# Down projection of an expert layer in column ranges of 512, 512, 384, 384, 256, gate products spread between pinned pairs of expert batches, and SBUF pools at other byte offsets

## The chip, the cores and the metric

The kernel runs on one NeuronCore of a Trainium2 chip. The metric is the device time of one execution in microseconds (us), the median of a few runs. Engines are named as the profile names them: PE is TensorE (matmuls; PEld its weight loads), DVE is VectorE, ACT is ScalarE, POOL is GpSimd, SP is SyncE, which only issues DMAs. SBUF is the on-chip memory that the engines read operands from, 128 partitions wide; PSUM is the small memory that PE accumulates into.

## The reference, cut to what matters

The program is two transformer blocks on 256 tokens of 2048 features. The first block (adaptive norm, three token mixers, a SwiGLU layer) and the mixer of the second are touched only by where their buffers lie. What the change rewrites is the end of the second block: a hierarchical mixture of 32 experts, and a gate on the whole residual.

```python
def hierarchical_moe(hn, w_router_group, w_router_expert, w_gate, w_up, w_down):
    ...   # group of the token, two experts in it, their weights: comb (tokens x 32)
    for e in range(N_EXPERTS):
        hid = jax.nn.silu(t @ w_gate[e]) * (t @ w_up[e])
        out = out + (hid @ w_down[e]).astype(jnp.float32) * comb[:, e:e + 1]

        h = h + hierarchical_moe(hn, ...)
        gate = jax.nn.sigmoid(rms_norm_2(h, ple_norm[i]) @ w_ple_gate[i])
        h = h + gate * (p[i] @ w_ple_up[i])
    return h
```

`w_down` is 32 x 256 x 2048 and `w_ple_gate` is 2048 x 2048, all fp32.

## The kernel before

**Dense layers.** Most of the time goes to products of fp32 data in three passes. `split` (lines 190 to 192) makes a rounded copy `whi` of a weight tile on ACT and the rest `wlo` on DVE; PE then adds `whi` by `xhi`, `wlo` by `xhi` and `whi` by `xlo` (lines 86, 87, 88), each a matmul of 128x128 stationary by 128x512 moving in the type fp32r. The stationary operand is the activations (`xhi`, `xlo`), the moving one the weights. In the output layer of the first block's feed-forward part the stationary tiles are called `hhi` and `hlo` and lie in another pool than all the others.

**Pools.** A pool with `side="right"` is laid down from the top of SBUF, the others from the bottom. The split weights, `xhi` and `xlo` and the weight buffers `w` lie in right pools; `hhi`, `hlo`, the expert weights `we` and the small scratch tiles (`junk`) in left ones. In the kernel before, the right pools start 480 bytes past a multiple of 512, the left ones 384.

**Router.** After the last column group of `w_out_2`, `residual_by4` adds the residual (L1227) and writes the sum `xr` in an interleaved order; `router_part` transposes it (L1246), scales it by the norm's gain into `xTg` (L1251, L1253) and multiplies by the router's weights (`plg`, L1255). `router` turns the logits (`lgs`, L1264) into expert slots by a chain of small DVE operations, to the one-hot matrices `S` (L1340), which gather the tokens of each expert (`pgx`, L1419).

**Experts.** `gate_up` computes four experts at a time, eight batches; `ph` (L1437) are its products. The ring of weight buffers (`wnext`) sets when SP may issue the next load: a load waits for the buffer's last reader.

**Down and gate.** `down` goes over ranges of output columns: 512, 512, 512, 256, 256. In a range, `Down.step(b)` loads the down weights of four experts, multiplies (`py`, L117), splits the result into `yh` and `yl`, and one batch later `combine` scatters it back to tokens (`pc`, L130 and L131). At a range's end the sum is added to the residual `yres` (L1491), transposed (`ptx`, L264) and split into `xqh` and `xql`. These are the inputs of the gate: `part(ri, g)` multiplies the range's rows of `w_ple_gate` into 512 output columns (group `g` of four; L1588 to L1590) and adds the result to `pacc` (L1601). The four groups of range `ri - 1` are hung between the batches of range `ri`. The groups of the last range (`last`) come after everything: products onto the running sum, then for each half `h` of the tokens the add (L1613; group 0 gets it from PE by an identity matmul, L1579), the sigmoid on ACT (L1614), times `up` (L1616) and plus `yres` (L1617), and the output DMA (L1618). The last two steps are on POOL for the second half of groups 0 to 2, else on DVE. The sigmoid needs `rmoe`, the norm over all columns.

**What sets the order.** A scheduler orders each engine's instructions by priorities; on PE nothing of this stage is pinned before the change. All weight loads are issued by SP in the order of the code.

Of the kernel before, what the change touches and what calls it, by code (L numbers as in the profile page):

```python
# [17 lines left out]
P = 128  # L18
T = 256
# [8 lines left out]
CAP = 32  # L28

# [61 lines left out]
class Down:  # L91
# [11 lines left out]
    def step(self, b):  # L103
        net, n, c0, pc = self.net, self.n, self.c0, self.pc
        nc = net.nc
        wd = net.a["w_expert_down_2"][0]
        hT, ST = self.hs[b]
        ne = min(4, 1024 // n)
        py = net.psm("py")
        wts = []  # L110
        for e0 in range(4 * b, 4 * b + 4, ne):
            wt = net.wnext()[:, :2 * ne * n].rearrange("p (e d) -> p e d", d=n)
            nc.sync.dma_start(wt, wd[e0:e0 + ne].rearrange("e (c p) d -> p (e c) d", p=P)[:, :, c0:c0 + n])
            wts.append(wt)
        for c in range(2):
            for e in range(4):
                nc.tensor.matmul(py[e * CAP:(e + 1) * CAP, :n], hT[:, c, e * CAP:(e + 1) * CAP],  # L117
                                 wts[e // ne][:, 2 * (e % ne) + c], start=(c == 0), stop=(c == 1))
        if self.ye is None:
            yh = net.wk.tile([P, 512], F32R, tag="yh", name="yh", bufs=2)  # L120
            yl = net.small.tile([P, 512], F32R, tag="junk", name="yl", bufs=2)
        else:
            yh, yl = (self.ye[:, 2 * i + b % 2] for i in range(2))
        net.split(yh[:, :n], yl[:, :n], py[:, :n])
        self.flush()

        def combine():
            for h in range(2):
                sl = slice(h * P, (h + 1) * P)
                nc.tensor.matmul(pc[h][:, :n], ST[:, sl], yh[:, :n], start=(b == 0), stop=False)  # L130
                nc.tensor.matmul(pc[h][:, :n], ST[:, sl], yl[:, :n], start=False, stop=(b == NE // 4 - 1))  # L131

        self.pending.append(combine)


class Net:
    def __init__(self, ctx, tc, a):
# [7 lines left out]
        self.pinned = False  # L145
# [44 lines left out]
    def split(self, hi, lo, src):  # L190
        self.nc.scalar.activation(hi, src, AF.Copy)  # L191
        self.nc.vector.tensor_tensor(lo, src, hi.bitcast(F32), op=ALU.subtract)  # L192
# [63 lines left out]
    def x_chunks(self, x, k0, nk=4):  # L256

        out = []
        for pr in range(0, nk, 2):
            pt = self.psm("ptx").rearrange("p (k t) -> p k t", k=2)  # L260
            for j in range(min(2, nk - pr)):
                k = k0 + pr + j
                for h in range(2):
                    self.nc.tensor.transpose(pt[:, j, h * P:(h + 1) * P], x[:, h, k * P:(k + 1) * P], self.ident)  # L264
# [3 lines left out]
    def x_split(self, x, k0, gain, X, nk=4, o=None):  # L268
# [3 lines left out]
        for pr, pt in enumerate(self.x_chunks(x, k0, nk)):  # L272
            for j in range(min(2, nk - 2 * pr)):
                k, d = k0 + 2 * pr + j, o + 2 * pr + j
                nc.scalar.activation(X[0][:, d], pt[:, j], AF.Copy, scale=gain[:, k:k + 1])
                nc.vector.scalar_tensor_tensor(X[1][:, d], pt[:, j], gain[:, k:k + 1], X[0][:, d].bitcast(F32),
                                               op0=ALU.mult, op1=ALU.subtract)
# [931 lines left out]
    def router_begin(self, rp):  # L1209
        nc, a = self.nc, self.a  # L1210
        self.wr = rp.tile([P, KD, 36], F32, name="wr")
        for c in range(4):
            rows = slice(512 * c, 512 * c + 512)
            for name, gs in (("w_router_group_2", slice(0, 4)), ("w_router_expert_2", slice(4, 36))):
                nc.scalar.dma_start(self.wr[:, 4 * c:4 * c + 4, gs],
                                    a[name][0][rows].rearrange("(p k) g -> p k g", k=4))
        self.lg = [self.psm("plg") for _ in range(2)]

    def residual_by4(self, x, cg, ps):
# [5 lines left out]
        for h in range(2):  # L1225
            t = self.small.tile([P, 512], F32, tag="junk", name="xr", bufs=2)
            nc.vector.tensor_tensor(t.rearrange("p (k q) -> p q k", k=4), ps[h].rearrange("p (q k) -> p q k", k=4),  # L1227
                                    x[:, h, sl].rearrange("p (q k) -> p q k", k=4), op=ALU.add)
            ts.append(t)

        def store():
            for h in range(2):
                nc.scalar.activation(ps[h], ts[h], AF.Square, accum_out=self.ssqp[:, h, cg:cg + 1])
                nc.gpsimd.tensor_copy(x[:, h, sl], ts[h])
# [3 lines left out]
    def router_part(self, rp, ts, cg):  # L1238

        nc = self.nc  # L1240
        for pr in range(2):
            pt = self.psm("ptx").rearrange("p (k t) -> p k t", k=2)
            for j in range(2):
                for h in range(2):
                    k = 2 * pr + j
# [524 lines left out]
```

## Time and profile before

| | us |
|---|---|
| median of 3 runs | 2657.91 (2655.55 to 2658.53) |
| profiled run, device time | 2652.12 |
| span of the profiled run, first to last instruction | 2650.4 |
| PE busy | 2496.7 (94%) |
| DVE busy | 1458.3 (55%) |
| ACT busy | 1034.6 (39%) |
| bytes read from HBM | 672.68 MB |

In time the program is a dense stretch to about 2074 us, the router to 2090, the experts' gate and up products to about 2420, the down projection with the gate's products to about 2606, and an end without weight loads to 2650.4. The busy time of PE is modelled from starts, so it overlaps itself a little; from start to start is the safer reading. A share of DMA over 1 means that all 16 engines had something in flight all the time.

### The profile page before, as it was taken

How to read it: one execution, taken by the hardware profiler on the slowest of the kernel's cores; microseconds unless marked ns; L12 is line 12 of the kernel's file. 1: busy time of each engine (PE TensorE's matmuls, PEld its weight loads, DVE VectorE, ACT ScalarE, POOL GpSimd, SP SyncE). 2: the span in 40 equal slices, each digit the busy share in tenths (PEclk: the TensorE clock that was granted, in tenths of full speed). 3: DMA queues.
4: the chain of work that ended last, by engine and by line, in shares of the span. 5: the costliest groups of instructions: out<-in, count | busy, mean ns of one | idle time of the engine just before them, and what ended most of it. 6: DMA issues, size and time to landing. Idle time of an engine off the chain costs nothing.

```text
span 2650.4 us, 31213 instructions
## 1 busy us (share of the span) xinstructions
PE 2496.7 (94%) x12275; PEld 1858.0 (70%) x12275; DVE 1458.3 (55%) x1935; ACT 1034.6 (39%) x1354; POOL 186.8 (7%) x251
## 2 busy tenths in 40 slices
PE   6999899999999999999999999999999887877997
PEld 3677788887887878778888888878778643332455
DVE  2668887787866567654554445557555311111345
ACT  3334445444455454344344444467444100001323
POOL 2212311000013000000000000012100000000001
PEclk9999999999999999999999999999999999999999
DMA  9975576788965557765555555555548799999994
GB/s 353 337 238 195 191 250 221 244 304 296 329 230 197 200 190 256 276 230 188 185 188 191 187 190 190 185 161 179 178 149 318 279 407 406 406 407 396 387 363 141
DMA packets 322757, 676.93 MB, mean 255 GB/s; under 512 B 22877, under 2 KB 46489, under 8 KB 322089
## 3 DMA queue, kind: packets, MB, share of 16 engines
q1 hardware_dynamic: 306408, 641.21, 68.9%
q0 software_dynamic: 8144, 27.82, 2.8%
q10 hardware_dynamic: 8048, 5.80, 0.7%
q8 instruction: 99, 1.62, 0.3%
q14 instruction: 58, 0.47, 0.0%
HBM read 672.68 MB, written 2.10 MB: 255 GB/s over the span
## 4 chain that ended last, share of the span: by engine, by line
PE 70%; DMA 15%; DVE 8%; ACT 3%; issue 2%; POOL 1%; SPq 1%; ACTq 0%; DVEq 0%; POOLq 0%
PE pd L87 18%; PE pd L88 18%; PE pd L86 18%; DMA we<-in_w_expert_up 6%; DMA w<-in_w_ada 4%; DVE wlo L192 3%; PE ph L1437 2%; DVE acc L386 2%; PE py L117 2%; DMA we<-in_w_expert_down 2%; ACT whi L191 1%; PE pgx L1419 1%; DMA w<-in_w_in 1%; PE ple L1588 1%; PE ple L1590 1%
## 5 line engine op out<-in xcount | busy, mean ns | idle before, releaser
L192 DVE TENSOR_TENSOR wlo<-w,whi 128x1024 fp32r<-128x1024 f32 x656 | 805.2, 1234 | 605.6 <-ACT whi L191 604.4
L191 ACT ACTIVATE whi<-w 128x1024 fp32r<-128x1024 f32 x656 | 690.9, 1059 | 945.4 <-PE pd L88 722.9
L87 PE MATMUL pd<-wlo,xhi 128*128 128x512 f32 x2272 | 894.8, 394 | 13.0 <-DVE wlo L192 12.7
L86 PE MATMUL pd<-whi,xhi 128*128 128x512 f32 x2272 | 899.2, 397 | 8.1 <-ACT whi L191 5.1
L88 PE MATMUL pd<-whi,xlo 128*128 128x512 f32 x2272 | 891.9, 393 | 0.0
L87 PEld LDWEIGHTS pd<-wlo,xhi 128*128 128x128 f32 x2272 | 428.8, 189 | 112.1 <-DVE wlo L192 24.6
L86 PEld LDWEIGHTS pd<-whi,xhi 128*128 128x128 f32 x2272 | 428.3, 189 | 109.4 <-ACT whi L191 13.7
L88 PEld LDWEIGHTS pd<-whi,xlo 128*128 128x128 f32 x2272 | 428.7, 189 | 92.4 <-issue 4.2
L1437 PE MATMUL ph<-we,xs 128*32 128x512 f32 x880 | 161.4, 637 | 46.5 <-DMA we<-in_w_expert_up 46.5
L386 DVE SCALAR_TENSOR_TENSOR acc<-w,sc,acc 128x512 f32<-128x512 f32 x240 | 180.9, 754 | 23.3 <-DMA w<-in_w_ada 18.7
L87 PE MATMUL pd<-wlo,hhi 128*128 128x512 f32 x352 | 140.4, 399 | 0.0
L86 PE MATMUL pd<-whi,hhi 128*128 128x512 f32 x352 | 139.2, 395 | 0.0
L88 PE MATMUL pd<-whi,hlo 128*128 128x512 f32 x352 | 138.0, 392 | 0.0
L1437 PEld LDWEIGHTS ph<-we,xs 128*32 128x32 f32 x880 | 39.6, 116 | 140.2 <-issue 128.2
L1421 DVE TENSOR_TENSOR xs<-pgx,ffng 128x512 f32<-128x512 f32 (+1 forms) x35 | 22.3, 645 | 163.9 <-PE pgx L1419 97.9
L117 PE MATMUL py<-we,ehT 128*32 128x512 f32 (+1 forms) x624 | 81.5, 515 | 4.3 <-DMA we<-in_w_expert_down 3.6
L86 PEld LDWEIGHTS pd<-whi,hhi 128*128 128x128 f32 x352 | 66.1, 188 | 16.8
L88 PEld LDWEIGHTS pd<-whi,hlo 128*128 128x128 f32 x352 | 66.1, 188 | 15.9
L87 PEld LDWEIGHTS pd<-wlo,hhi 128*128 128x128 f32 x352 | 66.1, 188 | 15.1
L1419 PEld LDWEIGHTS pgx<-S,xres 128*128 128x128 f32 x512 | 61.5, 197 | 15.1 <-issue 13.4
L191 ACT ACTIVATE own<-py 128x512 fp32r<-128x512 f32 x8 | 4.8, 597 | 163.0 <-PE py L117 163.0
L1419 PE MATMUL pgx<-S,xres 128*128 128x128 f32 x512 | 66.4, 285 | 0.7 <-DVE S L1340 0.7
(414 smaller groups left out, 1914.2 us busy)
## 6 DMA issues: line engine op xcount, KB each, us to landing
w<-in_w_in SPq DMA_DIRECT2D x142, 1024.0 KB
w<-in_w_ffn_in SPq DMA_DIRECT2D x88, 1024.0 KB
w<-in_w_ada SPq DMA_DIRECT2D x64, 1024.0 KB
we<-in_w_expert_down SPq DMA_DIRECT2D x62, 1024.0 KB
we<-in_w_expert_gate SPq DMA_DIRECT2D x110, 512.0 KB
we<-in_w_expert_up SPq DMA_DIRECT2D x110, 512.0 KB
w<-in_w_ffn_out SPq DMA_DIRECT2D x44, 1024.0 KB
w<-in_w_out SPq DMA_DIRECT2D x32, 1024.0 KB
```

What stands on the lines that cost most here:

```text
L86: nc.tensor.matmul(ps[h][:, :n], xhi[:, k0 + k, sl], hi[:, j, :n], start=(k == 0), stop=False)
L87: nc.tensor.matmul(ps[h][:, :n], xhi[:, k0 + k, sl], lo[:, j, :n], start=False, stop=False)
L88: nc.tensor.matmul(ps[h][:, :n], xlo[:, k0 + k, sl], hi[:, j, :n], start=False, stop=last)
L117: nc.tensor.matmul(py[e * CAP:(e + 1) * CAP, :n], hT[:, c, e * CAP:(e + 1) * CAP], wts[e // ne][:, 2 * (e % ne) + c], start=(c == 0), stop ...
L191: self.nc.scalar.activation(hi, src, AF.Copy)
L192: self.nc.vector.tensor_tensor(lo, src, hi.bitcast(F32), op=ALU.subtract)
L386: nc.vector.scalar_tensor_tensor(dst, wt[:, j], self.sc[:, kt + j:kt + j + 1], self.bias if kt + j == 0 else dst, op0=ALU.mult, op1=ALU.add)
L1419: nc.tensor.matmul(pg[:, j], src[:, h, k * P:(k + 1) * P], sb[:, h], start=(h == 0), stop=(h == 1))
L1421: nc.vector.tensor_tensor(xs[:, j:j + n], pg[:, j:j + n], self.ffng[:, 4 * kq + j:4 * kq + j + n, None].to_broadcast([P, n, P]), op=ALU.mult)
L1437: nc.tensor.matmul(ph[e * CAP:(e + 1) * CAP], xs[kq][:, k, e * CAP:(e + 1) * CAP], wt[:, :, k], start=(kk == 0), stop=(kk == KD - 1))
L1588: nc.tensor.matmul(ps[h], X[0][:, k, t], hi, start=(new and k == 0), stop=False)
L1590: nc.tensor.matmul(ps[h], X[1][:, k, t], hi, start=False, stop=(k == nk - 1))
```

## The change

What it does, part by part:

1. **Ranges.** `down` runs over 512, 512, 384, 384, 256 columns. A down weight row is then 2, 2, 1.5, 1.5 and 1 KB long (before: 2, 2, 2, 1, 1).
2. **Pairs.** `Down.step` takes two batches at once: the `py` products of both, then the splits, then the pending work, then both combines. PE's order in this stage is pinned to the code's order by `mm`. In the last pair the combines go half by half (`early`).
3. **Gate.** The parts of range `ri - 1` hang on pairs. Group 0 of the fourth range is left in PSUM (`held[0]`) and the last range's products for it go onto it; for groups 1 and 2 an identity matmul (`hold`) puts the running sum into PSUM before the last range is done. The last range's gate weights are loaded and split earlier (`wlast`): group 0's load stands before the last pair's, and the other three after. Groups 0 and 3 are added by DVE.
4. **End.** L1616 and L1617 become L1717 and L1718, all on DVE; the output DMAs are on SP; the sigmoid's table is loaded at the start of the stage (`warm`).
5. **Router.** `xr` is written in plain order, the transposes read it strided, the gain is multiplied into the router's weights once, there are two copies out of PSUM per column group instead of four, and the token weights (`weights`) come after the first one-hots.
6. **Pools.** A tile of 224 bytes (`edge`) lies at the top of SBUF and one of 96 bytes (`fill`) at the bottom, so that the right pools start 256 bytes past a multiple of 512 and the left ones at a multiple of 512.

The diff, cut to its core:

```diff
+EDGE, FILL = 56, 24
...
-    def step(self, b):
+    def step(self, b0, early=False):
...
+        if early:
+            self.flush()
+        for b in (b0, b0 + 1):
...
+                    net.mm(py[e * CAP:(e + 1) * CAP, :n], hT[:, c, e * CAP:(e + 1) * CAP],
+                           wts[e // ne][:, 2 * (e % ne) + c], start=(c == 0), stop=(c == 1))
+            pys.append((b, ST, py))
...
         self.flush()
 
         def combine():
-            for h in range(2):
+            bh = [(y, h) for y in ys for h in range(2)]
+            if early:
+                bh.sort(key=lambda t: t[1])
+            for (b, ST, yh, yl), h in bh:
...
+    def mm(self, *args, **kw):
+        i = self.nc.tensor.matmul(*args, **kw)
+        if self.pe_pinned:
+            self.tc.keep_in_program_order(i)
...
-            nc.vector.tensor_tensor(t.rearrange("p (k q) -> p q k", k=4), ps[h].rearrange("p (q k) -> p q k", k=4),
-                                    x[:, h, sl].rearrange("p (q k) -> p q k", k=4), op=ALU.add)
+            nc.vector.tensor_tensor(t, ps[h], x[:, h, sl], op=ALU.add)
...
+        nc.scalar.activation(xT[:, 0], pts[0], AF.Copy)
+        nc.vector.tensor_copy(xT[:, 1], pts[1])
...
-        ranges = [(0, 512), (512, 512), (1024, 512), (1536, 256), (1792, 256)]
+        ranges = [(0, 512), (512, 512), (1024, 384), (1408, 384), (1792, 256)]
...
+            def hold(g, pool):
+                held[g] = [pool("ple") for _ in range(2)]
+                for h in range(2):
+                    self.mm(held[g][h], self.ident, acc[:, h, g * 512:(g + 1) * 512], start=True, stop=False)
...
+                if b == 0:
+                    self.ring_is(["we"] * 8)
+                    late["next"] = part(ri - 1, 1)
+                if b == 2:
+                    late["next"] = part(ri - 1, 2)
+                if b == 6:
+                    wlast(0, True)
...
+                if b == 4:
+                    held[0] = [pdm("ple") for _ in range(2)]
+                    products(late[0], xq[end - 1], held[0], True, stop=False)
+                    flush()
+                if b == 6:
+                    wlast(1, True)
+                    hold(1, self.psm)
...
+                if ri == end:
+                    hold(2, pdm)
+                    wlast(2, True)
+                    tc.keep_in_program_order(nc.vector.tensor_reduce(ssq, self.ssqp, AX.X, ALU.add))
+                    self.rstd(r, ssq, D)
+                    wlast(3, True)
...
+                add = g in (0, 3)
+                ps = held[g] if g in held else [self.psm("ple") for _ in range(2)]
+                products(late[g], xq[end], ps, g not in held, g > 0)
+                for h in range(2):
+                    z = acc[:, h, sl]
+                    if add:
+                        nc.vector.tensor_tensor(z, ps[h], z, op=ALU.add)
+                    nc.scalar.activation(z, z if add else ps[h], AF.Sigmoid, scale=r[:, h:h + 1])
+                    nc.vector.tensor_tensor(z, z, up[:, h, sl], op=ALU.mult)
+                    nc.vector.tensor_tensor(z, z, y[:, h, sl], op=ALU.add)
+                    nc.sync.dma_start(ov[:, h, sl], z)
...
+        edge = ctx.enter_context(tc.tile_pool(name="edge", bufs=1, side="right"))
+        edge.tile([P, EDGE], F32, name="edge")
```

How PE's rows stand at the end of the program, from the last batch's `py` to the first products of the last range's gate. Before:

```order
L117 MATMUL py<-we,ehT 32x256 x8
L1588 MATMUL ple<-whi,xqh 128x512
L1589 MATMUL ple<-wlo,xqh 128x512
L1590 MATMUL ple<-whi,xql 128x512
L130 MATMUL pc<-yh,ST 128x256 x2
L1588 MATMUL ple<-whi,xqh 128x512
L131 MATMUL pc<-yl,ST 128x256 x2
```

After:

```order
L212 MATMUL py<-we,ehT 32x256 x16
L212 MATMUL ple<-pacc,kf 128x512 x2
L212 MATMUL pc<-yh,ST 128x256
L212 MATMUL pc<-yl,ST 128x256
...
L286 MATMUL ptx<-kf,yres 128x128 x4
L212 MATMUL ple<-pacc,kf 128x512 x2
L212 MATMUL ple<-wlast,xqh 128x512 x2
L212 MATMUL ple<-wlast,xql 128x512
```

Behind the last `py` stood twelve products of the range before last; now there stand one identity pair, the combines, the transposes, a second identity pair, and then the 48 products of the last range.

How DVE's rows stand at the very end (`pup` is the tile that `up` is in). Before, when POOL has six more of such rows:

```order
L192 TENSOR_TENSOR wlo<-we,whi 128x1024
L1613 TENSOR_TENSOR pacc<-ple,pacc 128x512 x3
L1616 TENSOR_TENSOR pacc<-pacc,pup 128x512
L1613 TENSOR_TENSOR pacc<-ple,pacc 128x512
L1617 TENSOR_TENSOR pacc<-pacc,yres 128x512
L1616 TENSOR_TENSOR pacc<-pacc,pup 128x512
L1617 TENSOR_TENSOR pacc<-pacc,yres 128x512
L1616 TENSOR_TENSOR pacc<-pacc,pup 128x512
L1617 TENSOR_TENSOR pacc<-pacc,yres 128x512
```

After:

```order
L1715 TENSOR_TENSOR pacc<-ple,pacc 128x512 x2
L1717 TENSOR_TENSOR pacc<-pacc,pup 128x512
L1718 TENSOR_TENSOR pacc<-pacc,yres 128x512
L208 TENSOR_TENSOR wlast<-we,wlast 128x1024
L1717 TENSOR_TENSOR pacc<-pacc,pup 128x512 x2
L1718 TENSOR_TENSOR pacc<-pacc,yres 128x512 x2
L1717 TENSOR_TENSOR pacc<-pacc,pup 128x512 x2
L1718 TENSOR_TENSOR pacc<-pacc,yres 128x512 x2
L1717 TENSOR_TENSOR pacc<-pacc,pup 128x512
```

DVE has six adds L1613 before and four L1715 after, and five each of L1616 and L1617 before and eight each of L1717 and L1718 after; the last seven rows (two adds, two L1717, three L1718) follow those shown.

How SP's rows stand, the last loads of the program. Before:

```order
L1568 DMA we<-in_w_ple_gate 128x2x512
L113 DMA we<-in_w_expert_down 128x8x256
L1568 DMA we<-in_w_ple_gate 128x2x512 x4
```

After:

```order
L1599 DMA we<-in_w_ple_gate 128x2x512
L119 DMA we<-in_w_expert_down 128x8x256 x2
L1599 DMA we<-in_w_ple_gate 128x2x512 x2
L1788 TENSOR_LOAD rounds
L1788 ISA x2
L1599 DMA we<-in_w_ple_gate 128x2x512
L1719 DMA out<-pacc 128x512 x8
```

Before, four gate loads follow the last down load; after, three do, and the outputs stand behind them on the same queue.

## Rows read from the trace of the kernel before

**Rows 1.** The page, the span in 40 equal slices.
```profile
DMA  9975576788965557765555555555548799999994
```

**Rows 2.** Windows by stage (us, busy, count, PEclk, DMA share, GB/s).
```profile
2100.00:2410.00 310.00, 251.12 (x1646) 116.39 (x1642) 41.61 (x97) 12.28 (x22) 0.00 (x0) 0.97 1.03 406
2420.00:2530.00 110.00, 100.08 (x488) 46.69 (x488) 38.04 (x47) 33.61 (x54) 0.00 (x0) 0.98 1.05 387
2530.00:2606.00 76.00, 71.86 (x470) 46.23 (x469) 34.81 (x50) 22.79 (x40) 0.00 (x0) 0.98 1.04 345
2606.00:2650.00 44.00, 28.59 (x157) 20.44 (x152) 26.93 (x38) 16.20 (x25) 9.83 (x8) 0.88 0.15 56
```

**Rows 3.** Timeline of the end, 2603 to 2651 (start, duration, what, idle before).
```profile
2603.69 0.37 SPq L1568 DMA_DIRECT2D we<-in_w_ple_gate  x1
...
2616.52 1.07 PE L117 MATMUL py<-we,ehT 128*32 128x256 f32 x16
...
2623.72 0.50 PE L1588 MATMUL ple<-whi,xqh 128*128 128x512 f32 x1 [0.56 <-ACT xqh L275]
...
2632.36 0.51 PE L1589 MATMUL ple<-wlo,xqh 128*128 128x512 f32 x1 [2.02 <-DVE wlo L192]
...
2633.95 0.63 PE L1588 MATMUL ple<-whi,xqh 128*128 128x512 f32 x1
...
2638.86 0.39 PE L1590 MATMUL ple<-whi,xql 128*128 128x512 f32 x1
...
2644.60 0.69 DVE L1617 TENSOR_TENSOR pacc<-pacc,yres 128x512 f32<-128x512 f32 x1
```

**Rows 4.** Groups by line and form, 2606 to 2651 (busy us, mean ns, idle before).
```profile
L192 DVE TENSOR_TENSOR wlo<-we,whi 128x1024 fp32r<-128x1024 f32 x6 | 7.3, 1220 | 1.0 <-ACT whi L191 1.0
...
L1616 POOL TENSOR_TENSOR pacc<-pacc,pup 128x512 f32<-128x512 f32 x3 | 4.8, 1591 | 8.2 <-ACT pacc L1614 8.2
L1617 DVE TENSOR_TENSOR pacc<-pacc,yres 128x512 f32<-128x512 f32 x5 | 4.5, 906 | 0.1
...
L1613 DVE TENSOR_TENSOR pacc<-ple,pacc 128x512 f32<-128x512 f32 x6 | 4.1, 688 | 3.3 <-PE ple L1590 3.3
L1614 ACT ACTIVATE pacc<-pacc,rmoe 128x512 f32<-128x512 f32 x6 | 4.1, 717 | 8.3 <-POOL pacc L1617 3.9 <-POOLq L1709 3.0 <-DVE pacc L1613 1.4
```

**Rows 5.** Timeline of the router.
```profile
2072.98 1.08 DVE L1227 TENSOR_TENSOR xr<-pd,xres 128x512 f32<-128x512 f32 x1 [4.55 <-PE pd L88]
...
2074.34 1.04 DVE L1227 TENSOR_TENSOR xr<-pd,xres 128x512 f32<-128x512 f32 x1 [0.28 <-PE pd L88]
...
2077.45 0.17 DVE L1296 COPY rmoe<-rstd 128x2 f32<-128x2 f32 x1 [0.38 <-POOL rstd L188]
...
2078.85 0.42 DVE L1264 COPY lgs<-plg 128x36 f32<-128x36 f32 x2 [0.50 <-PE plg L1255]
```

**Rows 6.** The page, costliest groups: dense products with either stationary tile.
```profile
L87 PE MATMUL pd<-wlo,xhi 128*128 128x512 f32 x2272 | 894.8, 394 | 13.0 <-DVE wlo L192 12.7
...
L87 PE MATMUL pd<-wlo,hhi 128*128 128x512 f32 x352 | 140.4, 399 | 0.0
```

**Rows 7.** Timeline of PE, dense products by `xhi` and `xlo`, first and last of ten.
```profile
1400.51 0.39 PE L86 MATMUL pd<-whi,xhi 128*128 128x512 f32 x1
...
1402.55 0.39 PE L86 MATMUL pd<-whi,xhi 128*128 128x512 f32 x1
```

**Rows 8.** Timeline of PE, dense products by `hhi` and `hlo`, first and last of ten.
```profile
1694.98 0.39 PE L86 MATMUL pd<-whi,hhi 128*128 128x512 f32 x1
...
1697.08 0.39 PE L86 MATMUL pd<-whi,hhi 128*128 128x512 f32 x1
```

**Rows 9.** Timeline of PE, products `ph` in plain fp32, one after another.
```profile
2424.85 0.61 PE L1437 MATMUL ph<-we,xs 128*32 128x512 f32 x2
...
2425.71 1.02 PE L1437 MATMUL ph<-we,xs 128*32 128x512 f32 x2
```

More of the change, by code (lines that the diff above doesn't have):

```diff
@@ L125, in step @@
+        ys = []
+        if self.ye is not None:
+            self.flush()
+        for b, ST, py in pys:
+            if self.ye is None:
+                yh = net.wk.tile([P, 512], F32R, tag="yh", name="yh", bufs=2)
+                yl = net.small.tile([P, 512], F32R, tag="junk", name="yl", bufs=2)
+            else:
+                yh, yl = (self.ye[:, 2 * i + b % 2] for i in range(2))
+            net.split(yh[:, :n], yl[:, :n], py[:, :n])
+            ys.append((b, ST, yh, yl))
         self.flush()
@@ L1329, in count @@
             nc.vector.tensor_copy(self.rounds, cm)
-        return S0, count
+        return S0, weights, count
     def one_hots(self, b):
@@ L1462, in gate_up, with down @@
         return out
-    def down(self, hs, src, dst, ranges, between=None, done=None, ahead=None, first=None):
+    def down(self, hs, src, dst, ranges, between=None, done=None, follow=None, first=None):
         nc = self.nc
@@ new lines, in part, with go @@
+            def part(ri, g):
+                parts = weights(ri, g)
+                def go():
+                    sl = slice(g * 512, (g + 1) * 512)
+                    ps = [self.psm("ple") for _ in range(2)]
+                    products(parts, xq[ri], ps, True)
+                    for h in range(2):
+                        if ri:
+                            nc.vector.tensor_tensor(acc[:, h, sl], ps[h], acc[:, h, sl], op=ALU.add)
+                        else:
+                            nc.scalar.activation(acc[:, h, sl], ps[h], AF.Copy)
+                return go
@@ new lines, in moe_ple, with pdm, wlast @@
+            held, late = {}, {}
+            def hold(g, pool):
+                held[g] = [pool("ple") for _ in range(2)]
+                for h in range(2):
+                    self.mm(held[g][h], self.ident, acc[:, h, g * 512:(g + 1) * 512], start=True, stop=False)
+            def pdm(name):
+                return self.pd.tile([P, 512], F32, tag="pd", name=name)
+            def wlast(g, pin=False):
+                if g == 0:
+                    room = self.xtp.tile([P, 2, 2, 2, 512], F32R, tag="xlo", name="wlast")
+                    late["room"] = [room[:, 0], room[:, 1]]
+                late[g] = weights(end, g, late["room"][g] if g < 2 else
+                                  self.wep.tile([P, 2, 2, 512], F32R, tag="we", name="wlast"), pin)
@@ L1627, in done @@
             def done(ri, pc):
                 c0, n = ranges[ri]
-                X = xq[ri] if ri in xq else xpair()
-                xq[ri] = X
-                self.x_split(y, c0 // P, self.pleg, X, n // P, 0)
-                self.ssq_part(y, ri, c0, n, pc)
-            def ahead():
-                xq["last"] = xq[len(ranges) - 1] = xpair()
-                tail.append(last(0))
-            ov = out[0].rearrange("(h p) d -> p h d", p=P)
-            self.down(hs, x, y, ranges, between, done, ahead, first)
@@ new lines, in done @@
+                if ri == end:
+                    hold(2, pdm)
[3 more added lines that the diff above has]
+                    wlast(3, True)
+            ssq = self.small.tile([P, 2], F32, tag="ssq", name="ssq")
+            r = self.small.tile([P, 2], F32, tag="rstd", name="rstd")
+            self.pe_pinned = True
+            self.down(hs, x, y, ranges, between, done, follow, first)
```

281 lines of the change are left out of this document (138 added, 143 removed).

## The prediction

> **What bounds the kernel now.** I read the strip of the span first: DMA is at 7 to 9 tenths in the first slices and again in the eight from slice 32 to 39, and at 5 to 6 in most between [rows 1]. The dense stretch to about 2074 us is therefore PE's: its products sit next to each other with 13 us of idle time in 2272 of them [rows 6]. From 2100 on the windows turn it round: DMA share 1.03 to 1.05 at 406, 387 and then 345 GB/s, until 2606 [rows 2]. There the loads set the pace, and time is won only at the ends. The last window is neither: 44 us with DMA at 0.15 and PE at 28.6 of 44 [rows 2]. The change can win there, in the router's 16 us ahead of the experts, and, through the addresses, in the dense stretch.
>
> In the end stretch I call E the landing of the last weight load. Its issue stands at 2603.69 [rows 3], and the window behind 2606 has little more than the outputs; I take E = 2606.5. The last `py` starts at 2616.52 [rows 3]. Four gate loads of 0.524 MB stand behind its weights in SP's order, 6.1 us at 345 GB/s, so these were there at about 2600.4: **PE runs 16 us behind the loads.** From that `py` to the first product on the last range is 7.20 us, the last product starts at 2638.86, the last DVE row ends at 2645.29, and the output takes 5.1 us to 2650.4 [rows 3]. So the end is E + 43.9.
>
> **The change part by part.**
>
> *Loads, and E.* The bytes are the same. The ranges of 384 turn 16.78 MB of 2 KB rows and 8.39 MB of 1 KB rows into 25.17 MB of 1.5 KB rows: 16,384 rows either way, so if a load costs a time per byte and a time per row, nothing changes. I take 0. By the nearest rows, 16.78/387 + 8.39/345 is 67.7 us; all at 345 it would be 73.0, at 387 65.0 [rows 2]. The bounds are 5.3 us lost and 2.7 won.
>
> *Is PE there in time?* After the change three loads follow the last down load: 1.57 MB, 4.1 us at 387 GB/s. PE has to catch up 16 us in the 186 us from 2420 to 2606. Its busy time there is 171.9 [rows 2], 14 us of room, and more than that, since a product counts as 0.39 where the next starts 0.23 later [rows 7]. Pairs also put a whole pair's `py` and the older pair's combine between a split and its use. I let PE be 1.2 us late; the bounds are 0 and 5.5.
>
> *The chain behind the last `py`.* Before it is 7.20 us with twelve products in it, which the change takes out, and one identity pair comes in. I keep 7.2. First product: E - 4.1 + 7.2 + 1.2 = E + 4.3. Then 48 products at 0.228 [rows 7], 2.7 us a group, the last at E + 15.2. The 2.02 us that PE waits for a `wlo`, and the rows of 0.63 behind it, at which the clock stood at its lower level (0.88 in the mean of the window) [rows 2, 3], go, as the gate's splits are done earlier. If the clock falls again, 12 products cost about 2.4 us, which DVE's backlog hides.
>
> *DVE becomes the last engine.* From the end of group 0 at E + 7.0 DVE has four adds, eight L1717 and eight L1718, at 0.69 each [rows 3, 4], and one split of 1.22 [rows 4]: 20 x 0.69 + 1.22 = 15.0 us, with 0.5 for hand-overs E + 22.5. PE was done 7 us sooner. Beside POOL these rows had a mean of 906 ns, and POOL took 1591 for one [rows 4], so DVE alone is not much worse than the two together; the sigmoids, 0.72 each [rows 4], keep ahead. With 5.1 us for the output the end is E + 27.6, against E + 43.9: **16.3 us won**, bounds 12.0 (PE 5.5 late) and 18.0 (not late, and no hand-over gaps). The output DMAs on SP stand behind loads that are long issued and cost nothing.
>
> *Router.* The second `xr` goes from 1.04 to about the 0.69 of a plain add, and there are fewer copies. But `lgs` at 2078.85 stands on DVE behind the copy of the norm, which ends at 2077.62 [rows 5]. So at most 1.2 us can be had; I take 0.6, and 0 as the other bound. The strided read by PE and the strided copy on POOL have no row; the transposes of the first half move in front of the last dense products, where PE's 0.23 steps cover DVE's 0.69.
>
> *Pairs in the gate and up stretch, and `up`.* They lie in a stretch at DMA share 1.03 with PE at 251 of 310 us [rows 2] and cost nothing; without that cover it would be one batch's `py` and combine, 3 us.
>
> *Addresses.* The stationary tiles `xhi` and `xlo` lie in the pools of the moving ones, `hhi` and `hlo` do not. Nine products take 2.04 us with the first (227 ns each) and 2.10 with the second (233) [rows 7, 8]; the page has 394 against 399 for the same row [rows 6]. Both are fp32r, 128x512, one after another at the full clock. What differs is where the stationary tile lies: 160 bytes off the moving one, modulo 256. After the change the two lie a multiple of 256 apart. I take it that the difference goes: 1056 products x 6.7 ns = **7.0 us**, bounds 0 and 7.0. All other products keep their distance, and I leave them at 227.
>
> The sum: 16.3 + 0 + 0.6 + 7.0 = 23.9 us from the profiled run's 2652.1, so 2628.2. The median of the runs shown is 5.8 us above that run; carried over, **2634**.
>
> **The rivals.**
>
> *Round addresses free all dense products.* 512 columns in 227 ns is 14 ns more than 512 cycles of the upper clock level, 213 ns. The `ph` rows in plain fp32, whose weights are in other pools, make two steps in 0.86 us [rows 9]; if one is two passes over 512 columns, a pass is 215 ns. No fp32r product of the trace has a moving tile on a multiple of 64 bytes, so nothing in it says whether the excess is the address or the type. If it is the address, 6816 x 12 + 1056 x 18 ns is 101 us in place of the 7: 2540. For it speaks that the distance of two tiles already matters; against it that plain fp32 with tiles at the same odd addresses loses nothing. 13%.
> [...]
>
> *Addresses do nothing.* The 6 ns are then from something else in that stretch. 2634 + 7 = 2641, 25%.
>
> *PE stays behind.* Pinning forbids PE to go around a wait. If that keeps the 16 us, the gain of the end falls by 14.8 to 1.5: 2649. The busy share of 71.86 in 76 us before the end [rows 2] speaks for it, the lower share earlier against it. 6%.
>
> *Slower: the new addresses are bad ones.* The products by `hhi` show that some distances cost 6.7 ns. If the new place of the right pools makes the 6816 others like these, that is 45.7 us, and the 7 are not won: 2634 + 7 + 46 = 2687. It decides from 3 ns a product on, where it eats the rest of the gain. No row has a tile at the new place; that the moving and the stationary tile of these products keep their distance speaks against it. 6%.
>
> **How the numbers follow.** The forecast gets 50%, and with the cases above 100%. Its terms' bounds add up to 6.7 and 28.9 us, 2651 and 2629 on the runs' median. I take 2652 for the high end. The low end I put at 2612, a sixth of the way to the first rival, for a part of that effect; the bulk of that rival and the slower one, 19%, stay outside. A measurement of this kernel can tell about 0.2% (5 us) from no change. Slower by more than that are the slower rival and little else, 5%; within it the worst of PE staying behind and a slow load, 4%; faster 91%.
>
> **What would show it.** The last L1718 some 22 us behind the last load, and DVE without idle time in its last 15 us, with PE done 7 us before: the end. The last `py` within 6 us of its weights: PE in time. The load rate in the ranges of 384, between 345 and 387 GB/s. Dense products from start to start: 227 with both kinds of stationary tile is the forecast, 233 with `hhi` no effect, 215 the first rival, over 230 everywhere the slower one. If the router's `lgs` comes no earlier after the last dense product than 5.0 us, its term is 0. The forecast is wrong if the end is as long as before with DVE waiting for PE, or if the dense stretch ends at another time than 7 us before 2074.

## The result

The changed kernel takes 2617.06 us (median of 4 runs, 2616.06 to 2617.83), against 2656.73 of the kernel before beside it: a ratio of 0.9851, 95% interval 0.9834 to 0.9868, some 40 us. The forecast was 2634, in a range from 2612 to 2652. The profiled run has a span of 2615.9 us, 34.5 less than the one before.

The strip of the span, the DMA engines' share and what they moved in 40 slices:

```profile
DMA  9966576788965557775555555555538699999995
GB/s 367 335 237 198 193 242 225 242 307 304 327 237 192 205 181 260 271 242 192 193 193 193 186 188 189 185 181 170 180 113 309 248 413 419 417 417 415 398 384 201
```

The shape is that of [rows 1]; what is new are the figures at the end, 413 to 419 GB/s. The windows by stage (us, busy and count of PE, PEld, DVE, ACT, POOL, then PEclk, DMA share, GB/s), the experts' gate and up products, two stretches of the down stage, the end:

```profile
2110.00:2380.00 270.00, 225.98 (x1444) 100.89 (x1440) 36.81 (x88) 11.21 (x20) 0.00 (x0) 0.95 1.03 418
2408.00:2488.00 80.00, 68.58 (x381) 37.39 (x382) 28.59 (x36) 30.17 (x50) 0.00 (x0) 0.98 1.05 399
2490.00:2565.00 75.00, 71.64 (x453) 47.40 (x452) 38.42 (x58) 25.28 (x43) 0.00 (x0) 1.00 1.04 384
```
```profile
2575.00:2615.00 40.00, 29.22 (x175) 20.95 (x173) 24.70 (x39) 14.19 (x24) 0.89 (x2) 0.90 0.28 98
```

Beside [rows 2] the loads of the first two stages are faster, 418 GB/s for 406 and 399 for 387. The 345 of the third row there takes in the last loads; as far behind the last `ph` as here the kernel before has 360 for the 384:

```profile
2515.00:2595.00 80.00, 74.81 (x450) 46.89 (x454) 35.93 (x49) 23.68 (x40) 0.00 (x0) 0.98 1.06 360
```

**That is the part that was not forecast.** The groups of the products by `hhi` answer to [rows 6], 389 ns for 399:

```profile
L88 PE MATMUL pd<-wlo,hhi 128*128 128x512 f32 x352 | 136.9, 389 | 0.0
```

The end, from the last pair's `py` on (start, duration, engine, line, idle before), answers to [rows 3]:

```profile
2567.41 1.23 SPq L119 DMA_DIRECT2D we<-in_w_expert_down  x2
...
2585.90 1.93 PE L212 MATMUL py<-we,ehT 128*32 128x256 f32 x32
...
2593.26 1.03 PE L212 MATMUL ple<-wlast,xqh 128*128 128x512 f32 x2
...
2595.96 1.36 DVE L1715 TENSOR_TENSOR pacc<-ple,pacc 128x512 f32<-128x512 f32 x2
...
2604.36 0.39 PE L212 MATMUL ple<-wlast,xql 128*128 128x512 f32 x1
...
2609.63 0.69 DVE L1718 TENSOR_TENSOR pacc<-pacc,yres 128x512 f32<-128x512 f32 x1
```

SP's row is the issue of the last two down loads; their `py` starts 18.5 us after it, so PE is still well behind the loads. From there the end takes 30.0 us, and DVE is the last engine, 5.6 us after PE.

The next table divides the profiled runs of all kernels below at five places, all starts of PE rows: the first dense product, the first and the last by `hhi`, the first and the last `ph`, the end of the span. Each number is the time from one of these places to the next, in us.

| kernel | to `hhi` | `hhi` | to `ph` | `ph` | last `ph` to end |
|---|---|---|---|---|---|
| before | 1205.1 | 471.5 | 387.0 | 335.7 | 224.3 |
| changed | 1200.0 | 464.4 | 391.5 | 322.4 | 212.2 |
| e1, before, round addresses | 1200.4 | 464.5 | 391.4 | 325.8 | 223.2 |
| e2, before, all at 128 | 1204.8 | 464.5 | 389.6 | 334.7 | 225.4 |
| e3, changed, old addresses | 1201.8 | 471.4 | 389.3 | 331.5 | 217.3 |
| e4, changed, old ranges | 1203.5 | 464.4 | 391.3 | 322.2 | 213.7 |
| e5, changed again | 1201.4 | 464.4 | 389.5 | 321.3 | 212.9 |
| e6, changed, POOL's rows back | 1199.8 | 464.4 | 392.1 | 322.2 | 214.4 |
| e7, changed, splits earlier | 1198.9 | 464.4 | 387.4 | 321.1 | 211.9 |
| e8, as e7, group 3 on PE | 1200.5 | 464.4 | 391.2 | 322.2 | 209.5 |
| e9, before, left pools moved | 1203.4 | 471.3 | 387.3 | 328.9 | 223.2 |
| e10, before, right pools moved | 1206.3 | 470.3 | 388.9 | 329.0 | 224.8 |
| e11, changed, old router | 1203.6 | 464.4 | 387.4 | 322.4 | 212.3 |
| e12, as e8, group 2's pair later | 1200.4 | 464.4 | 387.4 | 323.3 | 210.6 |

Between before and changed, 7.1 us lie in the `hhi` stretch, 13.3 between the `ph` and 12.1 behind them. The first column lies between 1198.9 and 1203.6 in the nine kernels with both pools at round places and between 1201.8 and 1206.3 in the other five, 3.3 us apart in the mean. The two groups overlap, and e10, whose right pools alone are round, has the longest of all. So a part of the 5 us between before and changed may be the addresses', but no run shows it. The third column's 4.5 us to the bad are mostly a fall of the clock that the run before did not have: in the window from 1900 to 1915 the granted clock was 0.77, in the same place of e11 and of the run before 1.00. Changed, then e11:

```profile
1900.00:1915.00 15.00, 13.52 (x51) 9.27 (x49) 8.05 (x19) 5.44 (x9) 0.00 (x0) 0.77 0.43 141
1900.00:1915.00 15.00, 13.51 (x63) 9.79 (x62) 9.03 (x18) 8.62 (x13) 0.00 (x0) 1.00 0.42 141
```

PE had waited 1.48 us for DVE there at 1902.8, and had short products in the microseconds after; it had the same wait in the run before. The other kernels follow it: the third column is 391 to 392 with 0.77 in this window (e1, e4, e6, e8), 389.5 to 389.6 with 0.89 (e2, e5), and 387.4 with 1.00 (e7, e11, e12).

### The profile page after: what moved, and what is told of

It reads as the page before. It is cut to its first block, busy times and chain, and to the rows that moved or that the text cites. A ratio compares the mean times of both kernels' runs of the same rounds, so it can differ in the third digit from the quotient of the medians.

```text
span 2615.9 us, 31259 instructions
## 1 busy us (share of the span) xinstructions
PE 2478.5 (95%) x12279; PEld 1862.2 (71%) x12279; DVE 1452.2 (56%) x1939; ACT 1035.3 (40%) x1355; POOL 179.0 (7%) x245
## 4 chain that ended last, share of the span: by engine, by line
PE 71%; DMA 15%; DVE 8%; ACT 2%; POOL 2%; issue 1%; SPq 1%; ACTq 0%; POOLq 0%; DVEq 0%
PE pd L88 19%; PE pd L89 19%; PE pd L87 19%; DMA w<-in_w_ada 4%; DMA we<-in_w_expert_down 3%; DMA we<-in_w_expert_up 3%; PE ph L1464 3%; PE ple L212 2%; DVE wlo L208 2%; DVE acc L413 2%; DMA we<-in_w_expert_gate 2%; PE pgx L1446 1%; PE py L212 1%; PE pad L812 1%; ACT whi L207 1%
## 5 line engine op out<-in xcount | busy, mean ns | idle before, releaser
L88 PE MATMUL pd<-wlo,xhi 128*128 128x512 f32 x2272 | 894.0, 394 | 11.5 <-DVE wlo L208 11.5
L88 PEld LDWEIGHTS pd<-wlo,xhi 128*128 128x128 f32 x2272 | 428.9, 189 | 109.5 <-DVE wlo L208 21.6
L88 PE MATMUL pd<-wlo,hhi 128*128 128x512 f32 x352 | 136.9, 389 | 0.0
L212 PE MATMUL py<-we,ehT 128*32 128x384 f32 (+2 forms) x608 | 75.2, 518 | 14.5 <-DMA we<-in_w_expert_down 12.2
L88 PEld LDWEIGHTS pd<-wlo,hhi 128*128 128x128 f32 x352 | 66.1, 188 | 13.5
```

The source lines that it names most:

```text
L88: nc.tensor.matmul(ps[h][:, :n], xhi[:, k0 + k, sl], lo[:, j, :n], start=False, stop=False)
L212: i = self.nc.tensor.matmul(*args, **kw)
```

## The experiments

**Addresses alone, and order alone.** Theory: two separate gains, the addresses through `hhi` and through the loads, and the rewritten end. Rival: the order of the code made the loads faster.

e1 is the kernel before with the fillers (the bottom one 32 floats long there, so that the pools stand as in the changed kernel):

```diff
+        self.cpool.tile([P, 32], F32, name="fill")
...
         self.pinned = False
+        self.cpool.tile([P, 32], F32, name="fill")
         return hT, raw
...
+        edge = ctx.enter_context(tc.tile_pool(name="edge", bufs=1, side="right"))
+        edge.tile([P, 56], F32, name="edge")
```

The filler's line stands in a second place of the code, too, here and in e9. It takes no further room: with 256 bytes the left pools would be 128 bytes off a multiple of 256, and the `hhi` stretch of e1, 464.5 us, is that of the changed kernel.

> The kernel before with the two filler tiles alone: right pools 256 bytes past a multiple of 512, left pools at one. Theory (addresses): the expert gate and up loads run at 416 GB/s as in the changed kernel (before 406) and the products by hhi start 227 ns apart (before 233); 7 us from the products, 10 to 13 us from the loads to the last ph, a few more from the down loads: ratio to before 0.990 to 0.993 (2631 to 2640 us). Rival (the rewritten order made the loads faster): loads stay at 406, only the 7 us are won, ratio 0.997.

Measured: 2631.56 us, ratio 0.9909 (0.9892 to 0.9926). Its windows of the gate and up products and of the first two parts of the down stage:

```profile
2110.00:2380.00 270.00, 224.51 (x1448) 101.77 (x1444) 36.99 (x88) 11.20 (x20) 0.00 (x0) 0.95 1.03 417
2412.00:2492.00 80.00, 75.00 (x358) 36.35 (x355) 27.74 (x34) 28.27 (x47) 0.00 (x0) 1.00 1.05 408
2497.00:2577.00 80.00, 75.13 (x474) 47.30 (x478) 36.53 (x51) 24.27 (x41) 0.00 (x0) 1.00 0.98 352
```

Not a line of the order is changed, and the loads run at 417 and 408 GB/s. The rival falls. But the last column of the table hardly moves: 224.3 to 223.2. The faster loads are lost later in the down stage, where the third window has 352 for the 360 before, and PE's waits there say why (line, releaser: us in total, times, longest):

```profile
PE pc L130 <- ACT yh L192: 6.7, 9, 1.7
PE pc L131 <- DVE yl L193: 2.6, 4, 1.0
PE ptx L265 <- DVE yres L1493: 2.1, 2, 1.5
PE ple L1591 <- DVE wlo L193: 2.0, 1, 2.0
```

They are the same as in the kernel before (6.7, 2.6, 2.1 and 2.0 there, too): PE waits for the split of the batch that it has just multiplied, not for loads.

e3 is the other half, the changed kernel with the pools back at their old places modulo 256 bytes:

```diff
-EDGE, FILL = 56, 24
+EDGE, FILL = 56, 56
...
-        edge = ctx.enter_context(tc.tile_pool(name="edge", bufs=1, side="right"))
-        edge.tile([P, EDGE], F32, name="edge")
```

> The changed kernel without the top filler and with another one at the bottom: the pools stand as in the kernel before, modulo 256 bytes (right 224, left 128). Theory (addresses and order are two separate gains): products by hhi at 233 ns, loads at 406 and 387 GB/s, and what is left is the end: 12 to 17 us of the 40, ratio to before 0.9935 to 0.9955. Rival (the order made the loads faster): ratio 0.988.

Measured: 2644.16 us, ratio 0.9961 (0.9949 to 0.9974). That is 9.1 us won, less than the 12 to 17 that were expected and further still from the rival's figure. The loads are back at 406 and 380 and the `hhi` stretch at 471.4:

```profile
2110.00:2390.00 280.00, 234.18 (x1494) 106.33 (x1485) 38.88 (x92) 11.67 (x21) 0.00 (x0) 0.95 1.03 406
2424.00:2504.00 80.00, 65.84 (x364) 34.55 (x365) 27.63 (x34) 29.39 (x48) 0.00 (x0) 0.98 1.04 380
```

PE's waits in the down stage of this kernel, and of the changed one:

```profile
PE py L212 <- DMA we<-in_w_expert_down: 17.1, 15, 1.6
PE pc L212 <- ACT own L207: 1.6, 2, 0.8
```
```profile
PE py L212 <- DMA we<-in_w_expert_down: 10.8, 12, 1.5
PE py L212 <- DVE xql L300: 2.3, 1, 2.3
PE pc L212 <- ACT own L207: 1.6, 2, 0.8
```

With pairs the waits for `yh` and `yl` are gone, and PE waits for loads, 17.1 us with the old addresses and 10.8 with the new. So in the stretch behind the last `ph` the addresses alone win 1.1 us, the order alone 7.0, and both 12.1: **each removes the wait behind which the other's gain is hidden.** In the whole time 21.7 and 9.1 us (medians beside their own kernel before) add up to 30.8, against 37.9 in e5 below; the intervals, 3 to 6 us wide each way, leave room for either.

Of the 13.3 us between the `ph`, e1 has 9.9. The other 3 to 4 are there in e3 as well, without faster loads; the down steps of the first range are hung differently there. I did not take that apart.

**Which addresses.** Theory: a load wants a destination at a multiple of 256 bytes; a dense product wants its stationary and its moving tile a multiple of 256 apart. e2 puts all pools at 384 past a multiple of 512, e9 moves only the left pools, e10 only the right ones:

```diff
+        edge.tile([P, 24], F32, name="edge")
```
```diff
+        self.cpool.tile([P, 32], F32, name="fill")
```
```diff
+        edge.tile([P, 56], F32, name="edge")
```

> The kernel before with one filler of 96 bytes at the top: left and right pools both 384 bytes past a multiple of 512, so all tiles lie at a multiple of 128 but not of 256, and the stationary tile a multiple of 256 from the moving one. Theory (loads want a multiple of 256, products want the distance): loads stay at 406 GB/s, products by hhi go to 227 ns: ratio 0.997. Rival (a multiple of 64 or 128 is enough for the loads, and the odd right pools spoilt the average): loads at 416, ratio 0.990 to 0.993.

Measured: 2644.2 us, ratio 0.9966 (0.9952 to 0.998).

> The kernel before with only the left pools moved to a multiple of 512 (right pools stay at 480). The expert weights' buffers we lie at a multiple of 256, the buffers w, wew and those of the dense layers do not; the stationary hhi is 32 bytes off the moving tile, modulo 256. Theory (each load goes by its own destination): gate and up loads at 413 to 416 GB/s, since most go to we; down loads at 400 to 408; products by hhi somewhere from 227 to 233 ns, which no run has shown. Rival (the pools have to be right together): loads at 406.

Measured: 2642.04 us, ratio 0.9956 (0.994 to 0.9973).

> The kernel before with only the right pools moved (256 past a multiple of 512, left pools stay at 384). Theory (each load goes by its own destination): gate and up loads near 408, down loads at 387 to 390, since most go to we; products by hhi, now 128 bytes off modulo 256, from 227 to 233 ns. If the dense stretch's loads matter anywhere, the first product by hhi starts some us earlier than before.

Measured: 2644.57 us, ratio 0.9965 (0.9951 to 0.9978). The windows of the three, gate and up and then the first part of the down stage, e2, e9 and e10 in this order:

```profile
2110.00:2390.00 280.00, 228.54 (x1466) 102.17 (x1464) 38.01 (x90) 11.20 (x20) 0.00 (x0) 0.95 1.03 407
2424.00:2504.00 80.00, 73.42 (x350) 34.68 (x347) 27.04 (x33) 27.19 (x46) 0.00 (x0) 1.00 1.05 387
```
```profile
2110.00:2390.00 280.00, 232.67 (x1499) 106.03 (x1498) 39.13 (x92) 11.68 (x21) 0.00 (x0) 0.94 1.03 413
2430.00:2510.00 80.00, 76.47 (x362) 37.50 (x363) 26.98 (x31) 24.70 (x39) 0.00 (x0) 1.00 1.05 406
```
```profile
2110.00:2390.00 280.00, 234.48 (x1518) 107.21 (x1512) 39.13 (x92) 11.67 (x21) 0.00 (x0) 0.95 1.03 413
2430.00:2510.00 80.00, 74.74 (x361) 36.04 (x354) 28.71 (x36) 27.25 (x43) 0.00 (x0) 1.00 1.05 395
```

At 128 nothing is won (407, 387): a multiple of 128 is not enough for a load. With one side at a multiple of 256 the gate and up loads are half way, 413, whichever side it is. I had expected 408 in e10, and 387 to 390 for its down loads. In the gate and up stretch 6 of the ring's 14 slots (from the first batch on) are in right pools, so 413 is what about half the loads give. The down loads go mostly to left slots (8 of 10): 406 with these moved, 395 with the others. Each load goes by its own destination.

The Trainium skill, "DMA: Bandwidth & Descriptors", section "How a descriptor splits into AXI transactions", says that a transaction has to start at a multiple of 256 bytes, and that a descriptor off one fetches bytes below its start that it does not use. It tells this of what a descriptor reads; here the destinations were moved. The runs agree in kind: 16 engines at 406 and 418 GB/s take 161 and 157 ns for a 4 KB row, at 387 and 408 85 and 80 ns for a 2 KB row, 4 to 5 ns per row in both. All these kernels read the same rows of the same inputs.

For the products by `hhi` e2 shows the distance by itself: 464.5 us with both tiles at 384, as with both at round places. With the distance at 32 (e9) and at 128 (e10) the stretch is 471.3 and 470.3, about as slow as at 160 before, and the lines of the group have nearly the same mean there, L88 with 395 in both (e9, then e10):

```profile
L86 PE MATMUL pd<-whi,hhi 128*128 128x512 f32 x352 | 139.7, 397 | 0.0
L87 PE MATMUL pd<-wlo,hhi 128*128 128x512 f32 x352 | 139.2, 395 | 0.0
```
```profile
L86 PE MATMUL pd<-whi,hhi 128*128 128x512 f32 x352 | 139.3, 396 | 0.0
L87 PE MATMUL pd<-wlo,hhi 128*128 128x512 f32 x352 | 138.9, 395 | 0.0
```

**The ranges.** e4 is the changed kernel with the old ranges:

```diff
-        ranges = [(0, 512), (512, 512), (1024, 384), (1408, 384), (1792, 256)]
+        ranges = [(0, 512), (512, 512), (1024, 512), (1536, 256), (1792, 256)]
```

> The changed kernel with the old column ranges 512, 512, 512, 256, 256. Theory (PE, not the loads, sets the end of the down stage, so a range's row length matters little): within 4 us of the changed kernel, ratio to before 0.984 to 0.987. Rival (the 1.5 KB rows are what keeps the loads fast): the range of 1 KB rows costs 6 us or more, ratio 0.988 or above.

Measured: 2621.44 us, ratio 0.9883 (0.9862 to 0.9904), 0.0032 above the changed kernel, which is past the bound that the theory gave and where the rival began; the interval covers both. In the profile, though, the place where ranges act is unmoved: 213.7 us behind the last `ph` for 212.2, and from the last pair's `py` to the end of DVE 24.3 us for 24.4; the 1.5 are in the landing of the last output. Most of the rest of its profiled run's 4.9 us is in the first column, where ranges have no part. The loads of the later ranges do run slower, 357 GB/s for 384 in the changed kernel:

```profile
2494.00:2570.00 76.00, 75.32 (x491) 53.15 (x490) 40.76 (x54) 28.04 (x43) 0.00 (x0) 1.00 0.97 357
```

The ranges ahead of them run faster, 408 for 399, and the way from the last `ph` to the last pair's `py` is 182.1 us for 182.2. So the rival's 6 us for rows of 1 KB are not in the trace. I leave it open whether the ranges win 1 or 5 us in the whole.

**The router.** e11 has the router's inputs as before (the token weights stay behind the first one-hots; no run takes that back):

```diff
-            nc.vector.tensor_tensor(t, ps[h], x[:, h, sl], op=ALU.add)
+            nc.vector.tensor_tensor(t.rearrange("p (k q) -> p q k", k=4), ps[h].rearrange("p (q k) -> p q k", k=4),
+                                    x[:, h, sl].rearrange("p (q k) -> p q k", k=4), op=ALU.add)
...
-            pt = self.psm("ptx").rearrange("p (k t) -> p k t", k=4)
+            pt = self.psm("ptx").rearrange("p (k t) -> p k t", k=2)
...
-        nc.scalar.activation(xT[:, 0], pts[0], AF.Copy)
-        nc.vector.tensor_copy(xT[:, 1], pts[1])
```

> The changed kernel with the router's inputs made as before (interleaved sum, transposes all behind the last dense product, four gained copies per column group). Theory (the router term is nil: the transposes moved in front of the last dense products lengthen the dense stretch by what the router wins): from the last product by hhi to the first ph the same within 1.5 us, ratio to before within 0.001 of the changed kernel's. Rival (the router's rewriting is worth the 0.6 to 1.2 us that were forecast, or more): that stretch 1 to 3 us longer than in the changed kernel.

Measured: 2615.75 us, ratio 0.9856 (0.9838 to 0.9873). The rewriting of the router's inputs is worth nothing that can be seen. The third column is 4.1 us shorter than in the changed kernel, past the 1.5 expected, but that is mostly the clock's: among the kernels with 1.00 in the window from 1900 to 1915, e11 has 387.4 and e7 and e12, with the new router, 387.4 as well. In the changed kernel the row of the transposes stands between two dense products:

```profile
2064.14 0.39 PE L87 MATMUL pd<-whi,xhi 128*128 128x512 f32 x1
...
2064.47 0.75 PE L1273 MATMUL ptx<-kf,xr 128*128 128x128 f32 x4
...
2064.98 0.47 PE L88 MATMUL pd<-wlo,xhi 128*128 128x512 f32 x1
```

The 0.84 us from the first to the third of these rows, where 0.23 is usual, is what the earlier transposes cost. What is moved in front of the last dense product is paid there.

**The end.** Theory: DVE's backlog behind group 0 sets the end; rival: PE. e5 is the changed kernel again, as the yardstick for the next three.

> The changed kernel itself on the chip of the three next ones, as their yardstick: ratio to before 0.983 to 0.987.

Measured: 2616.03 us, ratio 0.986 (0.9838 to 0.9882). e6 gives POOL its rows back:

```diff
-                    nc.vector.tensor_tensor(z, z, up[:, h, sl], op=ALU.mult)
-                    nc.vector.tensor_tensor(z, z, y[:, h, sl], op=ALU.add)
+                    e = nc.gpsimd if h and g < 3 else nc.vector
+                    e.tensor_tensor(z, z, up[:, h, sl], op=ALU.mult)
+                    e.tensor_tensor(z, z, y[:, h, sl], op=ALU.add)
```

> The changed kernel with the last two steps of the second half of groups 0 to 2 on POOL again, as before. Theory (DVE's backlog sets the end: it works without a pause from 2596 to 2610.3, six rows of 0.69 go away, but the rows beside POOL take 0.9 to 1.7): within 1.5 us of the changed kernel either way. Rival (POOL's rows of 1.3 to 2.0 us come free beside DVE): the end 2.7 us earlier, when PE and one group's rows are the bound.

Measured: 2620.03 us, ratio 0.9871 (0.9843 to 0.9899). From the last pair's `py` to the end of the span it is 31.9 us for 30.0: worse than the 1.5 us either way that were expected, and the rival's gain is not there. Its timeline shows DVE's rows beside POOL's:

```profile
2600.33 2.10 POOL L1718 TENSOR_TENSOR pacc<-pacc,pup 128x512 f32<-128x512 f32 x1 [2.40 <-ACT pacc L1716]
...
2602.51 1.62 POOL L1719 TENSOR_TENSOR pacc<-pacc,yres 128x512 f32<-128x512 f32 x1
```
```profile
2601.20 1.78 DVE L1718 TENSOR_TENSOR pacc<-pacc,pup 128x512 f32<-128x512 f32 x1
2603.01 1.67 DVE L1719 TENSOR_TENSOR pacc<-pacc,yres 128x512 f32<-128x512 f32 x1
2604.60 1.77 DVE L1718 TENSOR_TENSOR pacc<-pacc,pup 128x512 f32<-128x512 f32 x1
```

A row of DVE takes 0.69 alone and 1.63 to 1.78 beside one of POOL. Here the two engines together are slower on these rows than DVE alone.

e7 takes the split of group 3's weights out of the backlog, e8 two adds as well:

```diff
                 if b == 6:
                     wlast(0, True)
+                    wlast(1, True)
...
-                    wlast(1, True)
+                    wlast(2, True)
                     hold(1, self.psm)
...
                     hold(2, pdm)
-                    wlast(2, True)
+                    wlast(3, True)
...
-                    wlast(3, True)
```

> The changed kernel with the splits of the last gate weights pinned one place earlier each (group 1's before the last pair, group 3's before the norm). Theory (DVE's backlog behind group 0 sets the end): the 1.22 us row leaves the backlog and the end comes 1.2 us earlier, the rows L1715 to L1718 starting at the same time. Rival (PE sets the end): nothing, or later, if the splits now wait for their loads in front of the last pair.

Measured: 2615.29 us, ratio 0.9862 (0.9839 to 0.9885); from the last pair's `py` to the end 28.9 us for 30.0.

```diff
-                add = g in (0, 3)
-                ps = held[g] if g in held else [self.psm("ple") for _ in range(2)]
+                add = g == 0
+                if g == 3:
+                    hold(3, self.psm)
+                ps = held[g]
```

> The one before, and group 3's running sum goes into PSUM by an identity matmul, too, in place of two DVE adds. Theory (DVE sets the end): another 1.4 us off DVE's backlog, 1 to 1.4 us onto PE in front of group 3, the end 0.5 to 1.2 us earlier still, then bound by PE and the last group's sigmoid and two DVE rows. Rival (PE sets the end): 1 us later.

Measured: 2614.91 us, ratio 0.9857 (0.9833 to 0.9881); 28.4 us:

```profile
2585.06 1.93 PE L212 MATMUL py<-we,ehT 128*32 128x256 f32 x32
...
2605.29 0.39 PE L212 MATMUL ple<-wlast,xql 128*128 128x512 f32 x1
...
2607.16 0.69 DVE L1720 TENSOR_TENSOR pacc<-pacc,yres 128x512 f32<-128x512 f32 x1
```

Of 1.2 and 0.5 to 1.2 us expected, the profiles have 1.1 and 0.5. DVE did set the end, and in e8 it follows PE by 2.2 us only. The medians, 2616.03, 2615.29 and 2614.91, go the same way but are not apart by more than their intervals.

e12 moves group 2's identity pair behind group 0's and 1's products:

```diff
-                    hold(2, pdm)
...
-                if g == 3:
-                    hold(3, self.psm)
+                if g >= 2:
+                    hold(g, pdm if g == 2 else self.psm)
```

> The kernel with the early splits and group 3 held on PE, and with group 2's identity pair moved from before group 0's products to before its own. Theory (the first products wait only for xqh, DVE's backlog starts when group 0 ends): products and DVE's adds start 0.4 to 0.6 us earlier after the last py, the end as much earlier (26.3 us from the last py instead of 26.8 and, in the changed kernel, 28.4): the fastest of all, ratio to before 0.983 to 0.986. Rival (PE sets the end by then): no change against the one before.

Measured: 2615.02 us, ratio 0.9861 (0.9839 to 0.9883), 29.2 us from the last pair's `py` to the end for e8's 28.4. (The expectation counts from the start of the very last `py`, 1.5 us later: 27.7 where it has 26.3, for e8's 26.8.) A miss: with DVE's backlog gone PE is the bound, and the pair had stood mostly in time in which PE would have waited for `xqh`. The first product comes 0.6 us earlier, and the pair takes 1.3 in its new place. No version beat the changed kernel by more than the measurement can tell.

## Why the prediction held, and where it did not

- **What bounds the kernel.** Right: a dense stretch of PE, then loads, then an end that belongs to neither. The sentence that time is won "only at the ends" of the load-bound stretch was wrong, because the loads themselves could be made faster.
- **Loads: a step that failed.** The term was put at 0, with -5.3 and +2.7 as bounds. It priced the row lengths of the down loads and left out where rows land, though the change moves every buffer. Measured, 406 GB/s became 418 and 387 became 399 to 408; between the first and the last `ph` that is 9.9 us (e1), of 13.3 in all. The missing term is most of the 16 us by which the forecast's gain of 23.9 fell short of the 39.7 of the medians. It moved the result near the low end of the range, which had been set there for another effect of the same addresses: that the range held it is luck. (The low end is called a sixth of the way to the first rival; 17 of the 89 us from 2629 to 2540 are nearer to a fifth.) The shares of the gain were wrong, too. Addresses alone were to win 7.0 us and won 21.7 (e1); all the rest was to win 16.9 and won 9.1 by itself (e3).
- **PE in time: the other step that failed.** Put at 1.2 us late, bounds 0 and 5.5, with a last `py` within 6 us of its weights as the sign. The last down loads were issued between 2567.41 and 2568.64 and their `py` started at 2585.90. Behind them came the three gate loads of 1.57 MB, and the trace moves just that from 2575.4 on:

```profile
2575.40:2580.00 4.60, 4.60 (x40) 3.27 (x42) 2.22 (x4) 1.75 (x3) 0.00 (x0) 1.00 0.65 226
2580.00:2584.20 4.20, 4.20 (x32) 3.09 (x24) 3.14 (x6) 1.66 (x3) 0.00 (x0) 1.00 0.40 125
```

  So, by this estimate, the weights had landed at 2575.4, and PE was 10.5 us behind them; 17 us before the change, by the same reckoning. PE does not catch up: its last wait for a load (10.8 us in all) ends at 2546.0, and from there to its last product it stands still for 1.0 us in total. It is not the faster loads alone, since e3, with the old ones, is 8 us behind. PE, not E, became what the end hangs on; e4 fits with this, since the ranges change the loads and hardly PE's work.
- **The chain behind the last `py`.** Put at 7.2 us to the first product of the last range; 7.36 measured.
- **DVE as the last engine.** Put at 15.5 us from the end of group 0 to DVE's end, PE 7 us sooner; 14.4 us (2595.96 to 2610.32) and 5.6 measured, and e6 to e8 show the bound from three sides.
- **The end as a whole.** From the last `py` the sum gave 30.5 us (E - 2.9 to E + 27.6); 30.0 measured. But the 16.3 us were counted against E. The last weight row lands at 2607.9 before (the forecast took 2606.5) and at 2584.1 after. So the end went from E + 42.5 to E + 31.8, 10.7 us won; most of what is missing is PE's lateness, with its `py` at E + 1.8 in place of E - 2.9.
- **Router.** 0.6 put, 0 found (e11). The sign was there: `lgs` starts 4.29 us after the start of the last dense product, 5.01 before. But the transposes that were said to be covered by dense products displace them, by 0.61 us.
- **Products by `hhi`.** 7.0 put, 7.1 found, and e2 shows that it is the distance of the two tiles.
- **The rivals.** The dense products by `xhi` are as long as before (394 ns in the page for 394), so round addresses do not bring them to 215 ns; from start to start they take 227 at either address. The Trainium skill, "TensorE: Matmul & The Clock Gate", section "Back-to-back issue gap", gives 216 ns for 512 columns as the gap of a single matmul and 131 for one in a stream; the streams of this case are at neither. No slower rival came in. *PE stays behind* came true in part: of 17 us 10.5 were left, and the faster loads hid them in the sum.

## What to carry to other kernels

When a change moves buffers, price the new addresses for every reader and writer: the transfers that fill a buffer as well as the products that read it. In a load-bound stretch a few ns per row are per cents of the time, and filler tiles cost nothing.
A faster resource shows only where it is the one waited for: look at what the waits of the stage name before counting a gain, and try two changes together when each hides the other's wait.

## What the runs showed of the hardware

- Loads to SBUF rows that start on a multiple of 256 bytes ran at 417 to 418 GB/s with 4 KB rows and 399 to 408 with 2 KB rows; at 128 or 224 past one at 406 to 407 and 380 to 387. By 406 against 418 and 387 against 408 that is 4 to 5 ns more per row on an engine.
- An fp32r product of 128x128 by 128x512 started every 227 ns where the stationary and the moving tile lay a multiple of 256 bytes apart, and every 233 with 32, 128 or 160 over; where both lay made no difference.
- A 128x512 fp32 row of two SBUF operands took DVE 0.69 us alone and 1.6 to 1.8 beside a POOL row of the same kind, which took 1.3 to 2.1 itself.
